# Attention of two layers with both heads of a pair at once: scores in 64x64 array tiles, weighing by P in 128x64 column tiles

## The chip, the core and the metric

The kernel runs on one core of one Trainium2 chip. The metric is the device time of one execution in microseconds (us), and smaller is better. TensorE is called PE below, VectorE DVE, ScalarE ACT, GpSimd POOL, and SyncE, which issues the loads of the weights, SP.

## The reference, cut to what matters

The program computes a first block of four layers and a second block of one. Layers 0 and 3 of the first block mix with dilated attention, and only that mixer is touched. There are 256 tokens and 1024 features, and 16 heads of 64 features, each with three groups of q, k and v (dilations 1, 4 and 16).

```python
ATTN_GROUPS = ((128, 1), (512, 4), (2048, 16))

def dilated_attention_mixer(x, positions, w_qkv, w_o):
    qkv = (x @ w_qkv).reshape(B, S, 3, GH, HEAD_DIM)
    q = rope_partial(qkv[:, :, 0], cos, sin)
    k = rope_partial(qkv[:, :, 1], cos, sin)
    v = qkv[:, :, 2]
    for g, (window, dilation) in enumerate(ATTN_GROUPS):
        sl = slice(g * HEADS_PER_GROUP, (g + 1) * HEADS_PER_GROUP)
        o, l = dilated_group_attention(q[:, :, sl], k[:, :, sl], v[:, :, sl], window, dilation)
        outs.append(o)
        lses.append(l)
    alpha = jax.nn.softmax(jnp.stack(lses, axis=0), axis=0)
    o = jnp.sum(alpha[..., None] * jnp.stack(outs, axis=0).astype(jnp.float32), axis=0)
    return o.astype(x.dtype).reshape(B, S, ATTN_OUT_WIDTH) @ w_o
```

The softmax over the groups' log-sum-exps makes the three groups of a head one softmax over all their keys, and the kernel computes it so: one row of scores per query, one maximum, one sum.

## The kernel before, in words

All large products are made three times, with both operands split into a rounded part and what rounding left (hi and lo, lines 225 to 227 in mm3). Weights come as units through SP's queue into one of three raw buffers, ACT rounds them to hi (line 73) and DVE subtracts (line 76); there are four buffers of hi and lo.

An attention layer (attn_layer) works through eight pairs of heads, s = 0 to 7. The 256 tokens are two tiles, T = 0 and 1, of 128 each. Within a tile even tokens come before odd ones, so that the second and the third group each keep to one half, c = 0 or 1, of 64 queries. The projections of the next pair (gemm(s + 1)) are a generator that yields after every 12 products of 128x384, 12 times per pair, and the attention steps of the pair are hung into these slots by number (the dictionary events, filled by at(slot, step, ...)). With b = 12 s - 1, the three flip_qk steps (transposes of q and k into qkT, line 782) stand in slots b to b + 2. Each pair has four units u = 4 s + i, i = 2 T + hh, where hh is the head of the pair. A unit has four steps:

- scores (slot b + 3 i + 3): the first group's scores by one product over 64 rows and 128 columns of the array (line 798), the other two groups' by four products of 64x64, for each half c and group g (line 803), all into one PSUM bank. DVE adds the mask and takes the maximum (line 807), ACT takes the exponential and its sum (line 808), DVE the reciprocal (line 809).
- flip_p (two slots later): the transposes of P (line 817), two for T = 0 and four for T = 1, and ACT's copy to pT (line 819).
- weigh (one slot after flip_p): P times v. The first group is one or two full 128x128 products (line 827), the others are 128x64 column tiles, one column tile for each c (line 831). DVE scales by the reciprocal into half of osb (line 832).
- flip_o, after the second head of a token tile: one transpose of osb (line 837), and hi and lo of the output (hid).

Steps of one slot stand in the order in which the loops append them, so in slot b + 6 the weighing of unit 0 comes directly before the scores of unit 1, and so on. What is left of the last units (the list tail: flip_p and weigh of u = 30 and 31, flip_o) runs within the boundary to the next phase (Boundary.run, argument mid), between the end of the first token tile's output projection and the transposes of the next norm (line 306). A scheduler then sets the order on each engine by its own estimates, with the written order as its basis.

All temporary PSUM results rotate through four banks (tp_bank), accumulators through four others (acc_bank).

## Time and profile before

| | us |
|---|---|
| median of three runs | 2191.24 |
| lowest, highest | 2190.22, 2191.39 |
| span of the profiled execution | 2182.7 |
| PE busy in it | 2153.9 |
| DVE busy in it | 1523.4 |
| ACT busy in it | 1219.5 |

The runs' times include what lies around the span, 8.5 us at the median. In the rows of a timeline, the first two columns are the start and the time from the first start to the last end of what is merged in the row, so rows can overlap: matmuls are pipelined, and what a piece of work takes in line is the distance from its start to the start of the next row. A form such as 64*128 64x256 says that 64 rows by 128 columns of the array hold the weights, and 256 columns are streamed through 64 rows. The count of a float32 product is twice the number of the program's instructions, since each is recorded as two passes. Products of hi and lo parts, and transposes, have one.

### The profile page before, as it was taken

To read this page: it belongs to the slowest core of one execution; us is meant where nothing else is said; L and a number is where in the kernel's file an instruction comes from. 1 tells how busy PE (TensorE), PEld (TensorE's weight loads), DVE (VectorE), ACT (ScalarE), POOL (GpSimd) and SP (SyncE) were. 2 spreads that over 40 slices of the span, in tenths; PEclk is the share of its full clock that TensorE was granted. 3 is DMA by queue.
4 is the path that set the end of the run, shared out by engine and by line. 5 is a ranking of instruction groups with operands and counts; after the bars stand their busy time and mean duration, and the time that the engine had idled before them with its cause. 6 is when DMAs were issued, how large, how long until landed. Compare 5 with 4: busy or idle time off the path is not lost.

```text
span 2182.7 us, 39068 instructions
## 1 busy us (share of the span) xinstructions
PE 2153.9 (99%) x15262; PEld 2007.8 (92%) x15262; DVE 1523.4 (70%) x3710; ACT 1219.5 (56%) x2355; POOL 94.8 (4%) x130
## 2 busy tenths in 40 slices
PE   9999999999999999999999999999999999989999
PEld 8999989989999889799889999899989998969999
DVE  6655569957799669799665555589757655677763
ACT  6555566645476566576555555576554445665442
POOL 1000000000000001100000000000010002011000
PEclk9999999999999999999999999999999999999999
DMA  7444436554555553155544434445537445423543
GB/s 256 141 132 133 160 108 213 184 188 155 199 179 199 193 182 112 39 180 198 193 161 149 144 131 133 152 157 193 193 139 260 165 155 180 150 68 125 185 156 116
DMA packets 57433, 352.33 MB, mean 161 GB/s; under 512 B 7233, under 2 KB 7777, under 8 KB 29729
## 3 DMA queue, kind: packets, MB, share of 16 engines
q1 hardware_dynamic: 53136, 338.88, 45.0%
q0 software_dynamic: 3824, 10.78, 1.6%
q8 instruction: 120, 1.97, 0.4%
q14 instruction: 65, 0.52, 0.1%
q10 hardware_dynamic: 288, 0.18, 0.0%
HBM read 348.74 MB, written 3.22 MB: 161 GB/s over the span
## 4 chain that ended last, share of the span: by engine, by line
PE 56%; DVE 5%; ACT 1%; POOL 1%; issue 1%; POOLq 0%; ACTq 0%; DVEq 0%
PE acc L225 16%; PE acc L227 16%; PE acc L226 16%; DVE lo L76 1%; DVE cvh L1015 1%; DVE o L1015 1%; PE tp L798 1%; PE tp L803 1%; POOL s L243 1%; PE tp L1664 1%; PE tp L782 1%; PE tp L817 0%; PE tp L831 0%; PE tp L992 0%; PE tp L827 0%
## 5 line engine op out<-in xcount | busy, mean ns | idle before, releaser
L76 DVE TENSOR_TENSOR lo<-raw,hi 128x512 fp32r<-128x512 f32 (+2 forms) x1440 | 855.1, 632 | 298.4 <-ACT hi L73 294.0
L73 ACT ACTIVATE hi<-raw 128x1024 fp32r<-128x1024 f32 (+3 forms) x720 | 670.2, 964 | 417.8 <-PE acc L226 156.5
L225 PE MATMUL acc<-xhi,hi 128*128 128x256 f32 (+1 forms) x2432 | 688.0, 283 | 0.9 <-DVE u L515 0.5
L227 PE MATMUL acc<-xhi,lo 128*128 128x256 f32 (+1 forms) x2432 | 688.3, 283 | 0.0
L226 PE MATMUL acc<-xlo,hi 128*128 128x256 f32 (+1 forms) x2432 | 688.0, 283 | 0.0
L225 PEld LDWEIGHTS acc<-xhi,hi 128*128 128x128 f32 x2432 | 459.5, 189 | 2.1 <-ACT u L513 0.7
L227 PEld LDWEIGHTS acc<-xhi,lo 128*128 128x128 f32 x2432 | 460.0, 189 | 1.1 <-issue 0.9
L226 PEld LDWEIGHTS acc<-xlo,hi 128*128 128x128 f32 x2432 | 457.1, 188 | 0.8 <-issue 0.4
L225 PE MATMUL acc<-hi,xhi 128*128 128x384 f32 (+2 forms) x920 | 321.3, 349 | 1.5 <-ACT xhi L348 1.4
L227 PE MATMUL acc<-hi,xlo 128*128 128x384 f32 (+2 forms) x920 | 307.7, 334 | 0.0
L226 PE MATMUL acc<-lo,xhi 128*128 128x384 f32 (+2 forms) x920 | 306.4, 333 | 0.0
L225 PE MATMUL acc<-hi,hidh 128*128 128x512 f32 x480 | 191.6, 399 | 0.6 <-ACT hidh L230 0.6
L226 PE MATMUL acc<-lo,hidh 128*128 128x512 f32 x480 | 189.6, 395 | 0.0
L227 PE MATMUL acc<-hi,hidl 128*128 128x512 f32 x480 | 189.5, 395 | 0.0
L225 PEld LDWEIGHTS acc<-hi,xhi 128*128 128x128 f32 x920 | 172.8, 188 | 10.9 <-ACT xhi L348 3.7
L226 PEld LDWEIGHTS acc<-lo,xhi 128*128 128x128 f32 x920 | 173.3, 188 | 1.9
L227 PEld LDWEIGHTS acc<-hi,xlo 128*128 128x128 f32 x920 | 172.7, 188 | 2.3
L243 POOL TENSOR_TENSOR s<-s,neghalf 128x1 f32<-128x1 f32 (+5 forms) x56 | 42.3, 757 | 1596.9 <-DVE s L256 1468.5
L225 PEld LDWEIGHTS acc<-hi,hidh 128*128 128x128 f32 x480 | 90.4, 188 | 20.9 <-issue 0.9
L227 PEld LDWEIGHTS acc<-hi,hidl 128*128 128x128 f32 x480 | 90.4, 188 | 20.3
L226 PEld LDWEIGHTS acc<-lo,hidh 128*128 128x128 f32 x480 | 90.5, 189 | 18.5
L225 PE MATMUL acc<-hidh,hi 128*128 128x272 f32 (+1 forms) x352 | 100.6, 286 | 0.0
(342 smaller groups left out, 2638.0 us busy)
## 6 DMA issues: line engine op xcount, KB each, us to landing
raw<-in_ffn_w_in_dram SPq DMA_DIRECT2D x88, 1024.0 KB, 4.9
raw<-in_attn_w_qkv_dram SPq DMA_DIRECT2D x96, 768.0 KB, 4.3
raw<-in_ffn_w_out_dram SPq DMA_DIRECT2D x44, 1024.0 KB, 4.9
raw<-in_ffn_w_gu_dram SPq DMA_DIRECT2D x44, 1024.0 KB, 4.9
raw<-in_ffn_w_dn_dram SPq DMA_DIRECT2D x32, 704.0 KB, 4.1
raw<-in_sc_w_in_dram SPq DMA_DIRECT2D x16, 768.0 KB, 4.3
raw<-in_cc_w_pw_dram SPq DMA_DIRECT2D x12, 1024.0 KB, 4.9
raw<-in_attn_w_o_dram SPq DMA_DIRECT2D x8, 1024.0 KB, 5.0
```

What stands on the lines that cost most here:

```text
L73: nc.scalar.activation(hi[:, sl], raw[:, sl], AF.Copy)
L76: nc.vector.tensor_sub(lo[:, s2], raw[:, s2], hi[:, s2].bitcast(F32))
L225: nc.tensor.matmul(o, lhsT=lh[0], rhs=rh[0], start=first, stop=False)
L226: nc.tensor.matmul(o, lhsT=lh[0], rhs=rh[1], start=False, stop=False)
L227: nc.tensor.matmul(o, lhsT=lh[1], rhs=rh[0], start=False, stop=last)
L243: mark["pow"] = nc.gpsimd.tensor_tensor(r[:parts], m[:parts], neghalf[:parts, :w], op=ALU.pow)
L782: nc.tensor.transpose(tp[:, 256 * c2 + P * T:256 * c2 + P * T + P], qk[s, T][:, 2 * c:2 * c + 2, :].rearrange("p a b -> p (a b)"), ident)
L798: nc.tensor.matmul(sc[:, 0:nw], lhsT=t[rows, 0, ts_], rhs=t[rows, 3, 0:nw], start=True, stop=True)
L803: nc.tensor.matmul(half[:, g], lhsT=t[rows, 1 + g, P * T + 64 * c:P * T + 64 * c + 64], rhs=keys, start=True, stop=True)
L1015: nc.vector.scalar_tensor_tensor(d, x, w, other, op0=ALU.mult, op1=ALU.add)
L1664: nc.tensor.matmul(o[:, :P], lhsT=pT[:rows, i, :], rhs=vals[t][:rows, P * hd:P * hd + P], start=i == 0, stop=i == len(kts) - 1)
```

## The change

Both heads of a pair and token tile are now one step. scores(s, T) takes two banks, one for each head, and makes twelve products of 64x64 tiles: for the first group one per head and half c, over all nw keys (line 802; before one product of 64x128 per head), and for the other two groups as before (line 808). The loops run over hh and c innermost, so each product goes to another of the four quarters of the array than the one before it: head hh has its 64 features in partitions 64 hh, the half c of the queries goes to output partitions 64 c. weigh(s, T) makes all products in 128x64 column tiles, the first group's too, with c innermost (line 840), both heads into one bank; one DVE operation scales both (line 843), and there is one reciprocal for both (line 818). There are four buffers for ns instead of two, and three for pT instead of two. The steps' slots are new: scores at b + 3 and b + 9, flip_p four slots after the scores, weigh two slots after flip_p, flip_o one after weigh. The steps of T = 1 run into the next pair's slots. The diff also drops docstrings and comments all over the file, which are left out here.

```diff
-            for f, u in mid:
-                f(u)
+            for f, a in mid:
+                f(*a)
...
-        def scores(u):
-            s, T, hh = unit(u)
-            t, ts_, rows = qkT[s], slice(P * T, P * T + P), slice(64 * hh, 64 * hh + 64)
-            nw = P * (T + 1)
-            sc = tp_bank()
-            nc.tensor.matmul(sc[:, 0:nw], lhsT=t[rows, 0, ts_], rhs=t[rows, 3, 0:nw], start=True, stop=True)
-            for c in range(2):
-                half = sc[64 * c:64 * c + 64, nw:2 * nw].rearrange("p (t g u) -> p g t u", g=2, u=64)
-                for g in range(2):
-                    keys = t[rows, 4 + g, 0:nw].rearrange("p (t c u) -> p c t u", c=2, u=64)[:, c]
-                    nc.tensor.matmul(half[:, g], lhsT=t[rows, 1 + g, P * T + 64 * c:P * T + 64 * c + 64], rhs=keys,
-                                     start=True, stop=True)
-            ns = pool.tile([P, 512], F32, tag="ns", bufs=2, name=nm("ns"))
-            nmax, den, rd = small(), small(), small()
...
+        def scores(s, T):
+
+            t = qkT[s]
+            nw = P * (T + 1)
+            sc = [tp_bank() for _ in range(2)]
+            tiles = [(hh, c) for hh in range(2) for c in range(2)]
+
+            def part(hh, c):
+                return sc[hh][64 * c:64 * c + 64], t[64 * hh:64 * hh + 64], P * T + 64 * c
+
+            for hh, c in tiles:
+                o, x, q0 = part(hh, c)
+                nc.tensor.matmul(o[:, 0:nw], lhsT=x[:, 0, q0:q0 + 64], rhs=x[:, 3, 0:nw], start=True, stop=True)
+            for g in range(2):
+                for hh, c in tiles:
+                    o, x, q0 = part(hh, c)
+                    half = o[:, nw:2 * nw].rearrange("p (t g u) -> p g t u", g=2, u=64)
+                    keys = x[:, 4 + g, 0:nw].rearrange("p (t c u) -> p c t u", c=2, u=64)[:, c]
+                    nc.tensor.matmul(half[:, g], lhsT=x[:, 1 + g, q0:q0 + 64], rhs=keys, start=True, stop=True)
+            den, rd = small(2), small(2)
...
-        def weigh(u):
-            s, T, hh = unit(u)
-            if hh == 0:
-                osb[s, T] = pool.tile([P, P], F32, tag="osb", bufs=2, name=nm("osb"))
+        def weigh(s, T):
             o = tp_bank()
-            for t in range(T + 1):
-                nc.tensor.matmul(o[:, :64], lhsT=pT[u][:, t, :], rhs=v[s, t][:, hh, :], start=t == 0, stop=False)
-            for c in range(2):
-                rows = slice(64 * c, 64 * c + 64)
-                for t in range(T + 1):
-                    nc.tensor.matmul(o[rows, :64], lhsT=pT[u][:, T + 1 + t, rows], rhs=vx[s, t][:, c, hh, :], start=False, stop=t == T)
-            nc.vector.tensor_scalar(osb[s, T][:, 64 * hh:64 * hh + 64], o[:, :64], sm_[u][1], None, op0=ALU.mult)
+            for hh in range(2):
+                steps = [(t, v[s, t][:, hh, :], None) for t in range(T + 1)]
+                steps += [(T + 1 + t, vx[s, t], hh) for t in range(T + 1)]
+                for i, (j, vals, h2) in enumerate(steps):
+                    for c in range(2):
+                        rows = slice(64 * c, 64 * c + 64)
+                        nc.tensor.matmul(o[rows, 64 * hh:64 * hh + 64], lhsT=pT[s, T][hh][:, j, rows],
+                                         rhs=vals if h2 is None else vals[:, c, hh, :], start=i == 0, stop=i == len(steps) - 1)
...
+            if s:
+                at(b + 1, flip_p, s - 1, 1)
+                at(b + 3, weigh, s - 1, 1)
+                at(b + 4, flip_o, s - 1, 1)
+            at(b + 3, scores, s, 0)
+            at(b + 7, flip_p, s, 0)
+            at(b + 9, weigh, s, 0)
+            at(b + 9, scores, s, 1)
+            at(b + 10, flip_o, s, 0)
+        tail += [(f, (7, 1)) for f in (flip_p, weigh, flip_o)]
```

On PE, the first layer, first pair, before: the weighing of the first head of T = 1 and the scores of the second (tp is the PSUM bank written, v and vx are the values, pT the transposed P).

```order
L827 MATMUL tp_835<-v_497,pT_813 128x64
L827 MATMUL tp_835<-v_516,pT_813 128x64
L831 MATMUL tp_835<-vx_498,pT_813 64x64
L831 MATMUL tp_835<-vx_517,pT_813 64x64
L831 MATMUL tp_835<-vx_498,pT_813 64x64
L831 MATMUL tp_835<-vx_517,pT_813 64x64
L798 MATMUL tp_843<-qkT_533 128x256
L803 MATMUL tp_843<-qkT_533 64x2x64 x4
```

On PE now: the weighing of T = 1 of the first pair, with the scores of the second pair's T = 0 behind it.

```order
L840 MATMUL tp_936<-v_497,pT_885 64x64 x2
L840 MATMUL tp_936<-v_516,pT_885 64x64 x2
L840 MATMUL tp_936<-vx_498,pT_885 64x64 x2
L840 MATMUL tp_936<-vx_517,pT_885 64x64 x2
L840 MATMUL tp_936<-v_497,pT_892 64x64 x2
L840 MATMUL tp_936<-v_516,pT_892 64x64 x2
L840 MATMUL tp_936<-vx_498,pT_892 64x64 x2
L840 MATMUL tp_936<-vx_517,pT_892 64x64 x2
L802 MATMUL tp_955<-qkT_838 64x128 x2
L802 MATMUL tp_956<-qkT_838 64x128 x2
L808 MATMUL tp_955<-qkT_838 64x64 x2
L808 MATMUL tp_956<-qkT_838 64x64 x2
```

Where three forms followed each other (full array, column tiles, 64x128 and then 64x64), there are two, and each row's x2 is the pair of column tiles.

On ACT, first layer, from the second to the third pair, before: the copies of P of T = 1 (pT) between halves of weight splits (hi), evacuations of v (v, vx), the copy of transposed q and k (qkT) and the exponential (ns).

```order
L73 ACTIVATE hi_1255<-raw_1111 128x768
L819 ACTIVATE pT_1184<-tp_1179 128x512
L73 ACTIVATE hi_1255<-raw_1111 128x768
L715 ACTIVATE v_1198<-acc_1139,s_244 128x128
L715 ACTIVATE vx_1199<-acc_1139,s_244 64x128 x2
L788 ACTIVATE qkT_1227<-tp_1228 128x512
L808 ACTIVATE ns_1220,s_1222<-ns_1220,s_1221 128x512
L715 ACTIVATE v_1246<-acc_1140,s_260 128x128
L715 ACTIVATE vx_1247<-acc_1140,s_260 64x128
L73 ACTIVATE hi_1310<-raw_1169 128x768 x2
L715 ACTIVATE vx_1247<-acc_1140,s_260 64x128
L819 ACTIVATE pT_1288<-tp_1283 128x512
```

Now, at the same place:

```order
L73 ACTIVATE hi_1299<-raw_1180 128x768
L829 ACTIVATE pT_1256<-tp_1251 128x512
L715 ACTIVATE vx_1229<-acc_1151,s_260 64x128
L829 ACTIVATE pT_1263<-tp_1258 128x512
L73 ACTIVATE hi_1299<-raw_1180 128x768
L788 ACTIVATE qkT_1209<-tp_1279 128x512
L73 ACTIVATE hi_1385<-raw_1235 128x768 x2
L815 ACTIVATE ns_1342,s_1340<-ns_1342,s_1343 128x256
```

The two copies of P, which stood eleven rows apart, are next to each other but for one small copy.

On PE, at the end of the second attention layer, before: the tail between products of the output projection (acc).

```order
L817 MATMUL tp_15806<-ident,ns_15693 128x128 x4
L225 MATMUL acc_15663<-hi_15624,hidh_12844 128x512
L226 MATMUL acc_15663<-lo_15625,hidh_12844 128x512
L227 MATMUL acc_15663<-hi_15624,hidl_12845 128x512
L225 MATMUL acc_15663<-hi_15624,hidh_12844 128x512
L827 MATMUL tp_15814<-v_15482,pT_15811 128x64
L827 MATMUL tp_15814<-v_15530,pT_15811 128x64
L831 MATMUL tp_15814<-vx_15483,pT_15811 64x64
L831 MATMUL tp_15814<-vx_15531,pT_15811 64x64
L831 MATMUL tp_15814<-vx_15483,pT_15811 64x64
L831 MATMUL tp_15814<-vx_15531,pT_15811 64x64
L817 MATMUL tp_15822<-ident,ns_15742 128x128 x4
```

And now:

```order
L827 MATMUL tp_15804<-ident,ns_15702 128x128 x4
L827 MATMUL tp_15811<-ident,ns_15706 128x128 x4
L225 MATMUL acc_15661<-hi_15631,hidh_12844 128x512
L226 MATMUL acc_15661<-lo_15632,hidh_12844 128x512
L840 MATMUL tp_15818<-v_15486,pT_15809 64x64 x2
L840 MATMUL tp_15818<-v_15512,pT_15809 64x64 x2
L840 MATMUL tp_15818<-vx_15487,pT_15809 64x64 x2
L840 MATMUL tp_15818<-vx_15513,pT_15809 64x64 x2
L840 MATMUL tp_15818<-v_15486,pT_15816 64x64 x2
L840 MATMUL tp_15818<-v_15512,pT_15816 64x64 x2
L840 MATMUL tp_15818<-vx_15487,pT_15816 64x64 x2
L840 MATMUL tp_15818<-vx_15513,pT_15816 64x64 x2
```

The last two weighings with their transposes have become one step, and two projection products stand between transposes and weighing instead of four.

## Rows read from the trace of the kernel before

**Rows 1.** The page's first part: busy time, share of the span, instructions

```profile
PE 2153.9 (99%) x15262; PEld 2007.8 (92%) x15262; DVE 1523.4 (70%) x3710; ACT 1219.5 (56%) x2355; POOL 94.8 (4%) x130
```

**Rows 2.** Stretch, us; busy PE, PEld, DVE, ACT, POOL; granted clock, DMA share, GB/s

```profile
66.89:102.04 35.15, 35.15 (x247) 32.97 (x247) 20.16 (x56) 19.43 (x38) 0.00 (x0) 1.00 0.42 136
```

**Rows 3.** PE's timeline, 85.3 to 87.2 us: start, us, line, operands, form, count

```profile
85.29 0.33 PE L227 MATMUL acc<-hi,xlo 128*128 128x384 f32 x1
85.46 0.33 PE L827 MATMUL tp<-v,pT 128*128 128x64 f32 x2
85.72 0.34 PE L831 MATMUL tp<-vx,pT 128*64 128x64 f32 x4
85.98 0.48 PE L798 MATMUL tp<-qkT 64*128 64x128 f32 x2
86.39 0.46 PE L803 MATMUL tp<-qkT 64*64 64x64 f32 x8
86.78 0.44 PE L225 MATMUL acc<-hi,xhi 128*128 128x384 f32 x1
87.06 0.34 PE L226 MATMUL acc<-lo,xhi 128*128 128x384 f32 x1
```

**Rows 4.** PE's timeline, 93.3 to 95.5 us

```profile
93.37 0.33 PE L827 MATMUL tp<-v,pT 128*128 128x64 f32 x2
...
93.89 0.70 PE L798 MATMUL tp<-qkT 64*128 64x256 f32 x2
94.52 0.66 PE L803 MATMUL tp<-qkT 64*64 64x128 f32 x8
95.11 0.44 PE L225 MATMUL acc<-hi,xhi 128*128 128x384 f32 x1
```

**Rows 5.** PE's timeline, 76.8 to 79.3 us

```profile
77.07 0.55 PE L827 MATMUL tp<-v,pT 128*128 128x64 f32 x4
77.55 0.46 PE L831 MATMUL tp<-vx,pT 128*64 128x64 f32 x8
77.94 0.48 PE L798 MATMUL tp<-qkT 64*128 64x128 f32 x2
...
78.74 0.44 PE L225 MATMUL acc<-hi,xhi 128*128 128x384 f32 x1
```

**Rows 6.** PE's timeline, 66.6 to 69.8 us

```profile
66.90 0.55 PE L827 MATMUL tp<-v,pT 128*128 128x64 f32 x4
...
68.98 0.66 PE L782 MATMUL tp<-ident,qk 128*128 128x128 f32 x4
```

**Rows 7.** PE's timeline in the second block, 1877.7 and 1881.1 us

```profile
1877.76 0.52 PE L1690 MATMUL tp<-kaT,qaT 64*128 64x144 f32 x4
1878.21 0.38 PE L225 MATMUL acc<-xhi,hi 128*128 128x256 f32 x1
...
1881.21 0.76 PE L1690 MATMUL tp<-kaT,qaT 64*128 64x144 f32 x8
1881.90 0.39 PE L225 MATMUL acc<-xhi,hi 128*128 128x256 f32 x1
```

**Rows 8.** ACT's groups in one pair of heads: busy us, mean ns, idle before

```profile
L808 ACT ACTIVATE ns<-ns,s 128x512 f32<-128x512 f32 x2 | 1.4, 724 | 0.4 <-DVE s L807 0.4
...
L819 ACT ACTIVATE pT<-tp 128x512 f32<-128x512 f32 x2 | 1.2, 590 | 0.6 <-PE tp L817 0.6
```

**Rows 9.** What line 827 (weighing) waited for in the whole span: us, times

```profile
  ACT pT L819: 1.2, 4
```

**Rows 10.** PE's timeline at the first attention layer's end, 313.4 to 315 us

```profile
313.44 0.39 PE L225 MATMUL acc<-hi,hidh 128*128 128x512 f32 x1
313.67 0.40 PE L226 MATMUL acc<-lo,hidh 128*128 128x512 f32 x1
314.28 0.65 PE L306 MATMUL tp<-ident,xs 128*128 128x128 f32 x4 [0.21 <-ACT xs L332]
```

**Rows 11.** The page's second part: GB/s moved in 40 slices of the span

```profile
GB/s 256 141 132 133 160 108 213 184 188 155 199 179 199 193 182 112 39 180 198 193 161 149 144 131 133 152 157 193 193 139 260 165 155 180 150 68 125 185 156 116
```

## The prediction

> **What bounds the kernel now.** I read the busy times first: TensorE (PE) is busy 99% of the span [rows 1]. [...] The third view is PE's timeline around the attention products, where the start of one row to the start of the next is what that row costs in line [rows 3 to 6]. A 128x384 projection product starts every 0.17 us [rows 3]; 144 of them (3 parts, 2 halves, 2 token tiles, 4 k, 3 each) are 25.06 us at 0.174. The other 10.09 us of the period are attention. Of these, 24 transposes of q, k and P and two of the output stay as they are; the rest, scores and weighing, is what changes.

> **What that rest costs before.** Four times a pair, PE goes from projections into weighing, then scores, then back. With 0.11 us for the first projection after it (0.28 to the next instead of 0.17 [rows 3]) the four cost: weighing of T = 0 with scores of T = 0: 86.78 - 85.46 + 0.11 = 1.43 [rows 3]; with scores of T = 1: 95.11 - 93.37 + 0.11 = 1.85 [rows 4]; weighing of T = 1 with scores of T = 0: 78.74 - 77.07 + 0.11 = 1.78 [rows 5]; with scores of T = 1, running on into transposes (half of the 0.11): 68.98 - 66.90 + 0.05 = 2.13 [rows 6]. Sum 7.19 us a pair.

> **Unit prices.** Every float32 product stands in the trace as two passes (x8 for the four products of L803). One tile at a time: L798's two passes take 0.41 for 128 columns [rows 3] and 0.63 for 256 [rows 4], so 0.11 a pass per 128 columns. Two column tiles: L803's eight passes take 0.39 for 64 columns [rows 3] and 0.59 for 128 [rows 4], 0.20 for 512 more columns where L798 took 0.22 for 256 more. The two column tiles therefore already run side by side, although all products of c = 0 stand ahead of those of c = 1 in the program. L831: two pairs of passes 0.26 [rows 3], four pairs 0.39 [rows 5], so 0.065 a pair; L803's pairs of 64 columns grow by 0.05; I take 0.06. L827 in the full array: two more passes take 0.22 (0.48 against 0.26 [rows 5, 3]), 0.11 a pass of 64 columns, which as a stream need 0.055: it waits for its 128-column weight load. Row tiles side by side are nowhere in these layers, but L1690 of the second block alternates two of them: four passes of 144 columns take 0.45 to the next row, eight take 0.69 [rows 7]: 0.24 for 576 columns more, half of L798's price. Row tiles overlap too, where the program alternates them. Four tiles at once no row shows; the pairwise rows are the nearest, and I take four.

> **The change part by part.** *Weighing* both heads in column tiles: 16 pairs of passes for T = 1, 8 for T = 0: 0.26 + 14 x 0.06 = 1.10 and 0.26 + 6 x 0.06 = 0.62; the full-array form with its 0.11 a pass is gone, and with it the change of form inside. *Scores* in four tiles: each tile has two passes over all keys and four over half of them. T = 0: 0.39 (four of 64, [rows 3]) + 2 x 0.11 = 0.61; T = 1: 0.59 + 2 x 0.22 = 1.03. *Changes of array form*: sixteen a pair become six. The one from weighing to scores and the way back lie in the prices above; the way in from projections to column tiles is not in the trace: 0 as into L827 at 85.46, or 0.15 as from L827 to L831 (0.26 less two streams of 0.055) [rows 3]; I take 0.10. Sum: 0.10 + 1.10 + 0.61 + 0.11 = 1.92 and 0.10 + 0.62 + 1.03 + 0.11 = 1.86, together 3.78 instead of 7.19: 3.41 us less a pair, 54.6 us for 16 pairs in two layers.

> *Off PE.* DVE loses half of the reciprocals and of the output scalings (one of both heads each); ACT's exponentials and copies stay, 0.72 and 0.59 us for T = 1 [rows 8], but come two by two. Hidden cover: from flip_p to weigh it was one slot of 12 products, now two, 24 x 0.174 = 4.2 us, in which ACT has two copies, 1.18 us, with a half of a weight split and a small copy between them. Scores to flip_p: two slots became four. Before, PE waited there only 1.2 us in four places [rows 9]. The new shares, 19.43 and 20.16 of 31.7 us, are 61 and 64%. The weights for a pair then arrive at 136 x 35.15 / 31.74 = 151 GB/s, and the page has a slice at 260 [rows 11]. Buffers (ns 4, pT 3) and banks (14 a pair instead of 17 from the same four) are freed two slots or more before their next use. If that cover is gone, it is the rival on waits below. SP's and POOL's orders do not change.

> *The tail.* After the last projections of a layer the transposes of the next norm wait for ACT: these products follow each other by 0.23 us, the last before the transposes starts at 313.67, and the transposes begin at 314.28 [rows 10], 0.4 us late. The chain of norm steps behind it does not get shorter, so what the last weighing saves, some 0.9 us a layer, turns into wait: 2 us back. Net 52.6.

> The profiled span is 2182.7, so 2130.1; the runs' median is 8.5 above the span, which I keep: 2191.2 - 52.6 = **2138.6**. Its own range: entry free (-3.2), pairs at 0.05 (24 x 0.01 x 16 = -3.8), no loss in the tail (-2): 2129.6; entry 0.15 (+1.6), pairs at 0.065 (+1.9), scattered waits (+5): 2147.

> **Rivals.** *Two tiles at once, not four*: the array overlaps column tiles in 64x64 form, but takes row tiles in turn. Then T = 0 costs 4 x 0.05 + 2 x 0.11 = 0.42 more, T = 1 0.84 more: 1.26 x 16 = 20.2, 2159. Against: [rows 7], in the 64x128 form. [...]

> *Weight loads in the open.* If a column tile's load does not hide behind the other tile's product, each of 24 pairs and 12 groups of four a pair pays the half of L827's 0.11: 36 x 0.055 x 16 = 31.7 more, 2170. For it: L827 waits for its loads. Against it: L831's 0.065 a pair holds two loads and two streams of 0.055. [...]

> *Waits for the softmax*: both heads' copies are needed at once. At 0.3 (a wait of [rows 9]) to 0.59 (one copy, [rows 8]) for each of 32 weighings: 9.6 to 19 more, 2148 to 2158.

> *No overlap when tiles alternate* (the other side). Before, one column tile's products all precede the other's; now each product goes to another tile than the last. If that keeps them apart, a pair costs 24 x 2 x 0.055 = 2.64 to weigh, 1.76 + 3.52 for scores and 1.02 of changes, 8.94 instead of 7.19: +28, 2219. It decides once less than a third of the 5.2 us of overlap comes. Against: L1690 alternates and overlaps [rows 7].

> *Nothing moves*: something else than PE sets the period, about 2191; against it [rows 2].

> **How the numbers follow.** Forecast 0.75, two tiles 0.10, waits 0.06, loads 0.03, no overlap 0.04, nothing 0.02. The range runs from the forecast's low end to the two-tile case: 2130 to 2160. About 0.2% is what a measurement tells from no change: faster 0.94, same 0.02, slower 0.04.

> **What would show it.** A steady pair period near 31.7 us with PE busy throughout; weigh and scores groups of 1.9 us each; scores of T = 1 near 1.0 (1.9 if only two tiles run), passes in fours a few ns apart; 16 pairs of weigh passes in 1.1 (2.0 with open loads); PE waiting for P's copies would show as idle before the weighing; the wait before the norm's transposes near 1.3 us. Wrong is the forecast if the period stays over 33 us.

## The result, and the profile after

The changed kernel takes 2134.82 us, the median of four runs (2131.56 to 2138.26), beside 2191.31 for the kernel before in the same comparison: a ratio of 0.9744, with a 95% interval of 0.973 to 0.9758. The forecast was 2138.6 with a range of 2130 to 2160. Run again with the experiments (label a0_changed), the changed kernel took 2136.38 against 2190.34, 0.9754 (0.9739 to 0.9769).

The first rows of the profile after that answer to [rows 1] and [rows 2] are the page's busy times, and a stretch of one pair of heads in the first attention layer, from the weighing at 170.10 to the same weighing of the next pair at 201.81. The columns of the second are the stretch, its length, busy PE, PEld, DVE, ACT, POOL, granted clock, DMA share, GB/s.

```profile
PE 2104.3 (99%) x15582; PEld 1974.8 (93%) x15582; DVE 1507.8 (71%) x3646; ACT 1216.2 (57%) x2355; POOL 95.5 (4%) x130
```

```profile
170.09:201.80 31.71, 31.71 (x267) 30.51 (x266) 19.21 (x51) 19.10 (x38) 0.00 (x0) 1.00 0.44 150
```

PE is busy 99% of the span in both kernels, which says nothing of the 50 us between them. The stretch says it: a pair took 35.15 us [rows 2] and takes 31.71, and PE still has no gap in it.

In the timeline of PE after, the weighing of T = 1 with the scores of T = 0, and below it the weighing of T = 0 with the scores of T = 1, answer to [rows 3 to 6]. As there, what a piece takes in line is the distance from its start to the start of the next row.

```profile
169.83 0.34 PE L227 MATMUL acc<-hi,xlo 128*128 128x384 f32 x1
170.10 0.45 PE L840 MATMUL tp<-v,pT 128*64 128x64 f32 x8
170.38 0.40 PE L840 MATMUL tp<-vx,pT 128*64 128x64 f32 x8
170.61 0.40 PE L840 MATMUL tp<-v,pT 128*64 128x64 f32 x8
170.84 0.40 PE L840 MATMUL tp<-vx,pT 128*64 128x64 f32 x8
171.18 0.45 PE L802 MATMUL tp<-qkT 64*64 64x128 f32 x8
171.45 0.41 PE L808 MATMUL tp<-qkT 64*64 64x64 f32 x16
171.79 0.45 PE L225 MATMUL acc<-hi,xhi 128*128 128x384 f32 x1
172.07 0.34 PE L226 MATMUL acc<-lo,xhi 128*128 128x384 f32 x1
```

```profile
153.10 0.33 PE L227 MATMUL acc<-hi,xlo 128*128 128x384 f32 x1
153.36 0.34 PE L840 MATMUL tp<-v,pT 128*64 128x64 f32 x4
...
153.98 0.66 PE L802 MATMUL tp<-qkT 64*64 64x256 f32 x8
154.46 0.62 PE L808 MATMUL tp<-qkT 64*64 64x128 f32 x16
155.01 0.45 PE L225 MATMUL acc<-hi,xhi 128*128 128x384 f32 x1
```

The first group takes 1.08 for the 32 passes of the weighing (170.10 to 171.18) and 0.61 for the 24 of the scores (171.18 to 171.79). With 0.10 on the way in (0.27 from L227 to L840 instead of 0.17) and 0.11 on the way out (0.28 from L225 to L226) it is 1.90 us. The second takes 0.62 and 1.03, 1.85 us in all. Unmerged, the records show the scores' passes starting in fours 6 to 7 ns apart, the next four 109 ns later for 128 columns, and the weighing's in pairs 6 to 7 ns apart, a pair every 58 ns.

Where the time went is seen by cutting each trace at the starts of PE's 100th, 1800th, 6300th and 7900th product of lines 225 to 227, counted from zero (there are 12744 in each of these kernels). Between the first two cuts lies nearly all of the first attention layer, between the last two nearly all of the second. The rest begins with 149.5 us that still belong to the first block (149.5 to 149.6 in all twelve traces); behind them comes the second block. Times are us. "Before, again" is the kernel before, profiled once more (label b0_before).

| | span | start to 100th | attention 1 | between | attention 2 | rest |
|---|---|---|---|---|---|---|
| before | 2182.7 | 28.9 | 356.5 | 726.8 | 357.0 | 713.5 |
| before, again | 2189.6 | 31.0 | 356.8 | 727.2 | 357.0 | 717.5 |
| after | 2132.8 | 30.2 | 329.4 | 726.4 | 329.8 | 717.1 |
| after, again (a0_changed) | 2133.2 | 29.4 | 329.3 | 726.8 | 329.7 | 718.0 |

The two attention layers lost 27.1 and 27.2 us, 54.4 together, where the forecast had 52.6 net. Everything else is the same within what one kernel differs from itself. PE's visits to the attention products account for it: they cost 7.19 us a pair before, as the prediction adds them up, and 3.75 after, which is 55.0 us for 16 pairs, less some 1 us that comes back at the layers' ends (see the tail below).

### The profile page after: what moved, and what is told of

Same layout as the page of the kernel before. It is cut to its first block, busy times and chain, and to the rows that moved or that the text cites. A ratio compares the mean times of both kernels' runs of the same rounds, so it can differ in the third digit from the quotient of the medians.

```text
span 2132.8 us, 39626 instructions
## 1 busy us (share of the span) xinstructions
PE 2104.3 (99%) x15582; PEld 1974.8 (93%) x15582; DVE 1507.8 (71%) x3646; ACT 1216.2 (57%) x2355; POOL 95.5 (4%) x130
## 4 chain that ended last, share of the span: by engine, by line
PE 56%; DVE 5%; ACT 1%; POOL 1%; issue 1%; ACTq 0%; POOLq 0%; DVEq 0%
PE acc L225 17%; PE acc L227 17%; PE acc L226 17%; DVE lo L76 1%; DVE cvh L1024 1%; DVE o L1024 1%; POOL s L243 1%; PE tp L1673 1%; PE tp L840 1%; PE tp L782 0%; PE tp L1001 0%; PE tp L827 0%; PE tp L802 0%; PE tp L306 0%; ACT hi L73 0%
## 5 line engine op out<-in xcount | busy, mean ns | idle before, releaser
L227 PE MATMUL acc<-xhi,lo 128*128 128x256 f32 (+1 forms) x2432 | 690.4, 284 | 0.0
L226 PE MATMUL acc<-xlo,hi 128*128 128x256 f32 (+1 forms) x2432 | 690.1, 284 | 0.0
L225 PE MATMUL acc<-xhi,hi 128*128 128x256 f32 (+1 forms) x2432 | 689.8, 284 | 0.2 <-DVE u L515 0.2
L227 PEld LDWEIGHTS acc<-xhi,lo 128*128 128x128 f32 x2432 | 461.9, 190 | 1.1 <-issue 0.9
L225 PEld LDWEIGHTS acc<-xhi,hi 128*128 128x128 f32 x2432 | 461.4, 190 | 1.0 <-issue 0.4
L226 PEld LDWEIGHTS acc<-xlo,hi 128*128 128x128 f32 x2432 | 459.0, 189 | 1.0 <-issue 0.6
L225 PE MATMUL acc<-hi,xhi 128*128 128x384 f32 (+2 forms) x920 | 317.7, 346 | 1.5 <-ACT xhi L348 1.4
L227 PE MATMUL acc<-hi,xlo 128*128 128x384 f32 (+2 forms) x920 | 307.9, 335 | 0.0
L226 PE MATMUL acc<-lo,xhi 128*128 128x384 f32 (+2 forms) x920 | 306.6, 333 | 0.0
L225 PE MATMUL acc<-hi,hidh 128*128 128x512 f32 x480 | 190.7, 398 | 0.3 <-ACT hidh L230 0.3
L227 PE MATMUL acc<-hi,hidl 128*128 128x512 f32 x480 | 189.6, 395 | 0.0
L226 PE MATMUL acc<-lo,hidh 128*128 128x512 f32 x480 | 189.4, 395 | 0.0
L225 PEld LDWEIGHTS acc<-hi,xhi 128*128 128x128 f32 x920 | 172.8, 188 | 9.8 <-ACT xhi L348 3.2
L227 PEld LDWEIGHTS acc<-hi,xlo 128*128 128x128 f32 x920 | 172.7, 188 | 2.5
L226 PEld LDWEIGHTS acc<-lo,xhi 128*128 128x128 f32 x920 | 173.2, 188 | 1.9
L225 PEld LDWEIGHTS acc<-hi,hidh 128*128 128x128 f32 x480 | 90.5, 189 | 20.6 <-ACT hidh L230 0.5
L227 PEld LDWEIGHTS acc<-hi,hidl 128*128 128x128 f32 x480 | 90.4, 188 | 19.7
L226 PEld LDWEIGHTS acc<-lo,hidh 128*128 128x128 f32 x480 | 90.5, 188 | 19.3
L225 PE MATMUL acc<-hidh,hi 128*128 128x272 f32 (+1 forms) x352 | 100.6, 286 | 0.0
```

What stands on the lines that cost most here:

```text
L225: nc.tensor.matmul(o, lhsT=lh[0], rhs=rh[0], start=first, stop=False)
L226: nc.tensor.matmul(o, lhsT=lh[0], rhs=rh[1], start=False, stop=False)
L227: nc.tensor.matmul(o, lhsT=lh[1], rhs=rh[0], start=False, stop=last)
```

## The experiments

Shares of one edit are told below by the two attention stretches of the traces, which repeat within 0.3 us, and by the medians with their intervals. The first four runs (a0_changed and e1 to e3) stood beside the kernel before at 2190.34 us, the next four at 2189.69, the last two at 2190.25.

**The changed kernel again.** Nothing is edited; it is the standard for the rest.

> The changed kernel itself, to see how its span goes with the granted clock. In the first trace the two attention layers gave 53.3 us and the unchanged rest took 3.4 us back, all of it where the granted clock stood at 0.5 in the second block's mixer. Theory: the work in the attention layers takes the same time in every run, and runs differ by the clock in the unchanged part; a run whose mean clock is 0.001 higher is about 2 us shorter. Rival: the runs differ although the mean clock does not.

Measured: 2136.38 us, attention layers 329.3 and 329.7, the same as in the first trace to 0.1 us, as the theory has it. (The 53.3 us that it names are 54.4 by the table's cuts.) How the time goes with the mean clock these four runs cannot tell, since theirs is 0.992 or 0.993 throughout. The four runs of the first comparison can: from 2138.26 us at 0.992 to 2131.56 at 0.996 it is 1.7 us for 0.001, near the 2 expected.

**One part alone: weighing in column tiles, one head at a time.** The kernel before, with this edit:

```diff
-            for t in range(T + 1):
-                nc.tensor.matmul(o[:, :64], lhsT=pT[u][:, t, :], rhs=v[s, t][:, hh, :], start=t == 0, stop=False)
-            for c in range(2):
-                rows = slice(64 * c, 64 * c + 64)
-                for t in range(T + 1):
-                    nc.tensor.matmul(o[rows, :64], lhsT=pT[u][:, T + 1 + t, rows], rhs=vx[s, t][:, c, hh, :], start=False, stop=t == T)
+            for j in range(2 * (T + 1)):
+                for c in range(2):
+                    rows = slice(64 * c, 64 * c + 64)
+                    vals = v[s, j][:, hh, :] if j <= T else vx[s, j - T - 1][:, c, hh, :]
+                    nc.tensor.matmul(o[rows, :64], lhsT=pT[u][:, j, rows], rhs=vals, start=j == 0, stop=j == 2 * T + 1)
```

> The kernel before, with all weighing in column tiles, one head at a time, in the old slots; scores as before. Theory (0.06 us per pair of passes, 0.10 for the way in instead of 0.15 from the full array): T = 0 saves 0.04 us a unit, T = 1 0.145, 0.37 a pair of heads, 6 us in all: 2185. Rival, weight loads of column tiles in the open: 0.055 more for each of 24 pairs of passes, 21 us more than that, slower than before: 2206.

Measured: 2183.34 us, ratio 0.9969 (0.9957 to 0.998); the attention layers lost 3.1 us each. PE's timeline of this run, at the place of [rows 5]:

```profile
79.09 0.45 PE L830 MATMUL tp<-v,pT 128*64 128x64 f32 x8
79.37 0.40 PE L830 MATMUL tp<-vx,pT 128*64 128x64 f32 x8
79.71 0.48 PE L798 MATMUL tp<-qkT 64*128 64x128 f32 x2
```

The weighing takes 0.62 us (79.09 to 79.71) where it took 0.87 before (77.07 to 77.94 [rows 5]). Against this stands the way into column tiles: from the last projection product to the first pass it is 0.27 us here (78.82 to 79.09), where it was 0.17 into the full array (76.90 to 77.07). So the column tiles in place of the full array's products are worth 6 us of the 54, as expected, and no more.

**One part alone: scores in 64x64 tiles, one head at a time.** The kernel before, with the first group's product split in two and c made the inner loop:

```diff
-            nc.tensor.matmul(sc[:, 0:nw], lhsT=t[rows, 0, ts_], rhs=t[rows, 3, 0:nw], start=True, stop=True)
             for c in range(2):
-                half = sc[64 * c:64 * c + 64, nw:2 * nw].rearrange("p (t g u) -> p g t u", g=2, u=64)
-                for g in range(2):
+                q0 = P * T + 64 * c
+                nc.tensor.matmul(sc[64 * c:64 * c + 64, 0:nw], lhsT=t[rows, 0, q0:q0 + 64], rhs=t[rows, 3, 0:nw], start=True, stop=True)
+            for g in range(2):
+                for c in range(2):
+                    half = sc[64 * c:64 * c + 64, nw:2 * nw].rearrange("p (t g u) -> p g t u", g=2, u=64)
```

> The kernel before, with all scores in 64x64 tiles, one head at a time (two column tiles, one row tile), in the old slots; weighing as before. Theory: T = 0 takes 0.61 us instead of 0.80, T = 1 1.03 instead of 1.22, 0.19 each for 64 units: 12 us, 2179. Rival: the first group's product gains nothing from being halved, since both halves read the same keys: 2191.

Measured: 2177.95 us, ratio 0.9945 (0.993 to 0.996); the attention layers lost 5.7 us each, 11.5 together, near the 12 of the theory.

**Both parts, one head at a time.** The two edits together; what is missing of the change is that the heads come in pairs.

> Both edits of the forms, one head at a time in the old slots. Theory: the sum, 18 us, 2173; what is left to the changed kernel, about 36 us, then is the pairing of heads (four tiles at once, half as many ways in and out). Rival: the forms alone give most of it, below 2155.

Measured: 2170.26 us, ratio 0.9909 (0.9893 to 0.9926); the attention layers lost 18.9 us together. PE's timeline of this run, one head's weighing and one head's scores of T = 0:

```profile
86.69 0.34 PE L832 MATMUL tp<-v,pT 128*64 128x64 f32 x4
86.85 0.29 PE L832 MATMUL tp<-vx,pT 128*64 128x64 f32 x4
87.07 0.44 PE L800 MATMUL tp<-qkT 64*64 64x128 f32 x4
87.34 0.40 PE L805 MATMUL tp<-qkT 64*64 64x64 f32 x8
87.66 0.44 PE L225 MATMUL acc<-hi,xhi 128*128 128x384 f32 x1
```

The two forms give a third of the gain. The other 35.5 us (54.4 less 18.9) come with the pairing of the heads and its new slots, which the next run takes apart.

**The pair's scores in two tiles instead of four.** The changed kernel, with both heads' scores from the same rows of the array:

```diff
-                return sc[hh][64 * c:64 * c + 64], t[64 * hh:64 * hh + 64], P * T + 64 * c
+                return sc[hh][64 * c:64 * c + 64], t[0:64], P * T + 64 * c
```

> The changed kernel, but the scores of both heads are made from the first head's rows (the second head's scores are left out, the first's made twice), so that the four products of a round stand in two tiles of the array and not four; all else as it was. Theory: only two tiles run at once, T = 0 takes 0.42 us longer and T = 1 0.84, 1.26 a pair of heads, 20 us: 2155. Rival: row tiles do not run side by side in 64x64 form anyway or something else gave the gain: 2135.

Measured: 2156.41 us, ratio 0.9838 (0.9822 to 0.9855); the attention layers take 339.6 and 340.2 us, 20.7 more than in the changed kernel. PE's timeline of this run, the scores of T = 0 and of T = 1:

```profile
77.96 0.65 PE L802 MATMUL tp<-qkT 64*64 64x128 f32 x8
78.44 0.63 PE L808 MATMUL tp<-qkT 64*64 64x64 f32 x16
79.00 0.44 PE L225 MATMUL acc<-hi,xhi 128*128 128x384 f32 x1
...
92.94 1.08 PE L802 MATMUL tp<-qkT 64*64 64x256 f32 x8
93.85 1.04 PE L808 MATMUL tp<-qkT 64*64 64x128 f32 x16
94.82 0.44 PE L225 MATMUL acc<-hi,xhi 128*128 128x384 f32 x1
```

The same products with the same columns take 1.04 and 1.88 us where four tiles take 0.61 and 1.03. So passes in four quarters of the array do run side by side here, and that is 20.7 us of the 35.5. The 14.8 left are argued from rows and not from a run of their own: per pair and token tile, two trips into attention become one. By the starts of its rows, a pair's visits cost 5.96 us with one head at a time (the run before) and 5.03 in this run, which is 14.9 us for 16 pairs, so next to nothing is left for the new slots and buffers. The rows also price a single trip. Two heads' weighings of T = 0 one by one are 2 x 0.38 (86.69 to 87.07 in the run before), together 0.62; two heads' scores in two tiles are 2 x 0.59 (87.07 to 87.66) one by one and 1.04 together. With 0.09 to 0.10 in and 0.11 out, one trip less is 0.14 + 0.14 + 0.10 + 0.11 = 0.49 us, and 32 of them 15.7, an estimate that comes out 0.9 high.

**The heads' scores one after the other.** The changed kernel with all six products of one head ahead of those of the other; the four tiles are the same:

```diff
-            for hh, c in tiles:
-                o, x, q0 = part(hh, c)
...
-            for g in range(2):
-                for hh, c in tiles:
+            for head in range(2):
+                mine = tiles[2 * head:2 * head + 2]
+                for hh, c in mine:
+                    o, x, q0 = part(hh, c)
...
+                for g in range(2):
+                    for hh, c in mine:
```

> The changed kernel with the scores' loops turned: all six products of the first head, then all six of the second, instead of head and half innermost. Theory: the array looks far enough ahead in its queue to start the second head's rows while the first head's still run, as it did with the halves before: 2135, the first products of the two heads some 40 ns apart. Rival: it works in order, and heads in turn run one after the other: up to 20 us more, 2155.

Measured: 2148.02 us, ratio 0.9807 (0.9793 to 0.9822); attention layers 335.3 and 335.9, 12.1 us more than in the changed kernel. Neither theory named this size. The queue is the expectation's word; what the trace shows is when passes start. PE's timeline of this run, the scores of T = 1 (L804 is the first product of each tile, L810 the other two):

```profile
156.89 0.65 PE L804 MATMUL tp<-qkT 64*64 64x256 f32 x4
157.38 0.28 PE L810 MATMUL tp<-qkT 64*64 64x128 f32 x2
157.39 0.43 PE L804 MATMUL tp<-qkT 64*64 64x256 f32 x2
157.48 0.39 PE L810 MATMUL tp<-qkT 64*64 64x128 f32 x4
157.66 0.38 PE L804 MATMUL tp<-qkT 64*64 64x256 f32 x2
157.70 0.77 PE L810 MATMUL tp<-qkT 64*64 64x128 f32 x10
158.40 0.44 PE L225 MATMUL acc<-hi,xhi 128*128 128x384 f32 x1
```

The second head's first passes (157.39) do not start with the first head's (156.89), and they do not wait for its last either. Each tile has six passes: two of L804 and four of L810. The second head starts 5 ns after the first head's two tiles have begun their third pass each (157.38, x2), that is, when three passes are left to start in each, and from there on passes of both heads start among each other (157.38 to 157.70). All 32 score groups of this trace have this order, for 128 columns (T = 0) as for 256.

**The halves of the queries one after the other.** The changed kernel with c as the outer loop of the weighing:

```diff
-                for i, (j, vals, h2) in enumerate(steps):
-                    for c in range(2):
-                        rows = slice(64 * c, 64 * c + 64)
+                for c in range(2):
+                    rows = slice(64 * c, 64 * c + 64)
+                    for i, (j, vals, h2) in enumerate(steps):
```

> The changed kernel with the weighing's loops turned: for each head all products of the half c = 0, then those of c = 1, instead of the halves in turn. Theory: as with the old line 831, the two column tiles run side by side all the same: 2135. Rival: they run one after the other: 24 times 0.05 us a pair of heads, 19 us more, 2154.

Measured: 2141.57 us, ratio 0.9773 (0.9758 to 0.9788); attention layers 332.5 and 333.0, 6.4 us more. Again neither theory named this size. PE's timeline of this run, the weighing of T = 1 (eight passes to the one column tile, eight to the other, for each head):

```profile
170.59 0.45 PE L840 MATMUL tp<-v,pT 128*64 128x64 f32 x4
170.87 0.22 PE L840 MATMUL tp<-vx,pT 128*64 128x64 f32 x1
170.88 0.27 PE L840 MATMUL tp<-v,pT 128*64 128x64 f32 x1
...
171.73 0.40 PE L840 MATMUL tp<-vx,pT 128*64 128x64 f32 x4
172.06 0.45 PE L802 MATMUL tp<-qkT 64*64 64x128 f32 x8
```

The other tile's first pass (170.88, L840 from v) starts 7 ns after the first tile's fifth of eight (170.87, from vx), again when three passes are left to start. The weighing takes 1.47 us instead of 1.08. The weighing of T = 0, whose runs are four passes long, lost only 0.04: its whole group takes 1.89 instead of 1.85. The two runs agree in a count, taken for each tile: the first pass for an idle tile started when three passes were left to start in each busy one, three in all where one tile was busy (e5), six where two were (e4). The kernel before fits it as well: its runs to one tile (L803, L831) are of four passes at most, and at 77.55 and 78.36 of its trace, unmerged, the two tiles' first passes start 13 ns apart. The theory of the next run is the author's estimate from these counts, which are of starts alone; no record shows a pass that waits.

**Runs of two products.** The changed kernel with the weighing in runs of two products, four passes:

```diff
-                for i, (j, vals, h2) in enumerate(steps):
+                for lo in range(0, len(steps), 2):
                     for c in range(2):
                         rows = slice(64 * c, 64 * c + 64)
-                        nc.tensor.matmul(o[rows, 64 * hh:64 * hh + 64], lhsT=pT[s, T][hh][:, j, rows],
...
+                        for i, (j, vals, h2) in list(enumerate(steps))[lo:lo + 2]:
+                            nc.tensor.matmul(o[rows, 64 * hh:64 * hh + 64], lhsT=pT[s, T][hh][:, j, rows],
```

> The changed kernel, with the weighing's products ordered in runs: two products (four passes) to the one column tile, two to the other, and so on, where e5_halves_in_turn gave up to four products (eight passes) in a row to one tile. Theory: a tile takes one running and three waiting passes, and only the fifth that comes while four are there holds up everything behind it. Runs of four passes then cost nothing: the group of T = 1's weighing takes 1.90 to 1.95 us as in the changed kernel, the attention layers 329.4 to 330.0 us, the median 2135 to 2138. Rival: there is no such limit, each run keeps the two tiles from overlapping in proportion to its length (0.38 us per group for runs of eight passes, nothing for runs of two): 0.13 us more in each of 16 groups, 2.03 us a group, 2 us more in all, attention layers 330.4.

Measured: 2136.35 us, ratio 0.9747 (0.973 to 0.9764); the group of T = 1 takes 1.93 us, that of T = 0 1.89; the attention layers take 330.4 and 330.8. PE's timeline of this run:

```profile
172.12 0.46 PE L841 MATMUL tp<-v,pT 128*64 128x64 f32 x8
172.40 0.45 PE L841 MATMUL tp<-vx,pT 128*64 128x64 f32 x8
...
173.25 0.45 PE L802 MATMUL tp<-qkT 64*64 64x128 f32 x8
```

The weighing takes 1.13 us: 0.05 more than in the changed kernel, not the 0.13 of the rival, and not the 0.38 of runs of eight. The group and the median lie where the theory put them. But the layers are 1.0 us longer, above the theory's 330.0 and at the 330.4 that the rival had named: runs of four cost some 0.04 us a group (16 groups in a layer, 0.6 us), and another 0.4 us a layer I cannot place. Unmerged, the second tile starts its last pass 54 ns behind the first; with c innermost both tiles' last passes start 7 ns apart. A run of four is nearly free, not free, and this run alone would not decide between the two; what speaks for a limit is where the idle tiles start in e4 and e5.

**The cover halved.** The changed kernel with flip_p one slot ahead of weigh instead of two:

```diff
-                at(b + 1, flip_p, s - 1, 1)
+                at(b + 2, flip_p, s - 1, 1)
...
-            at(b + 7, flip_p, s, 0)
+            at(b + 8, flip_p, s, 0)
```

> The changed kernel with flip_p one slot later, so one slot (12 products, 2.1 us) ahead of the weighing instead of two. Theory: ACT has two copies of 0.59 us and up to two halves of a weight split of 0.84 us in that time, so PE waits some tenths before the weighing: 0.3 us for one of two weighings a pair, 5 us, 2140. Rival: the second slot was not needed, 2135.

Measured: 2137.12 us, ratio 0.9757 (0.9742 to 0.9772); attention layers 329.7 and 329.7, 0.3 us more than in the changed kernel. What line 840 (weighing) waited for from ACT in the whole span (us, times), in this run and then in the changed kernel, answers to [rows 9]:

```profile
  ACT pT L829: 1.4, 4
```

```profile
  ACT hi L73: 0.7, 2
  ACT pT L829: 0.7, 2
```

In both it is 1.4 us in four places; in the changed kernel two of them are put down to another of ACT's operations. One slot, 2.1 us of projections, already hides ACT's two copies (0.59 us each for T = 1, 0.37 for T = 0 in the changed kernel's trace), as the rival had it. The second slot changes nothing that the medians can show.

**The kernel before, profiled again.** Nothing is edited. The question was what the 8.5 us between the first profile's span and the median were.

> The kernel before, profiled again; nothing is changed in it. Question: what are the 8.5 us by which the median of its runs lies over the span of its first profile? Theory: they are not around the span. Every run of the kernels so far exceeds its own span by 1.9 us, so an ordinary run of the kernel before has a span of 2186 to 2190 at a mean granted clock of 0.993 to 0.996, and the profile shows where: stretches at a granted clock of 0.5 in the second block, whose mixer is the same in both kernels, while the four layers of the first block take the same as in the first profile (attention layers 356.5 and 357.0 us from their 100th to their 1800th projection product). Rival: the second block keeps the full clock in this kernel and the span is again 2182 to 2184; then the change itself brings the slow stretches into the second block and costs 3 to 4 us there.

Measured: 2191.49 us with a span of 2189.6, 1.9 us apart. The core's span and mean granted clock in this run (2182.7 and 0.997 in the first profile of before), and then two stretches of the second block in the first profile and in this one (columns as in [rows 2]):

```profile
core 0: 2189.6 us, clock 0.993
```

```profile
1920.00:1930.00 10.00, 9.99 (x58) 7.45 (x58) 7.76 (x36) 6.52 (x27) 0.93 (x1) 1.00 0.01 2
1990.00:2000.00 10.00, 9.66 (x78) 9.27 (x79) 7.52 (x18) 5.08 (x8) 1.25 (x3) 1.00 0.56 198
```

```profile
1920.00:1930.00 10.00, 9.19 (x42) 7.68 (x44) 4.80 (x22) 3.81 (x17) 1.18 (x2) 0.66 0.10 43
1990.00:2000.00 10.00, 8.42 (x60) 8.22 (x59) 9.04 (x19) 5.38 (x11) 4.46 (x6) 0.84 0.31 105
```

The theory holds in the main. The same program had a granted clock of 1.00 throughout both stretches in one execution, and of 0.66 and 0.84 on the mean in the other (the work stands some 3 us later in it), and the rest, with the second block, took 717.5 us instead of 713.5. That is 4.0 of the 6.9 us between the two spans. Another 2.1 lie before the 100th product, which the theory did not name: from 10.3 to 13.7 us the granted clock is 0.51 in this run and 1.00 in the first. The changed kernel's profile has the like in its second block:

```profile
1860.00:1890.00 30.00, 26.53 (x118) 18.36 (x119) 21.02 (x101) 17.00 (x60) 4.57 (x5) 0.83 0.17 54
```

So the slow stretches are not the change's doing. What brings the clock down there in one execution and not in another stays open.

## Why the prediction was right, by its steps

**The bound.** Right: PE's products set the end of the attention stretches, and what they lost the span lost. The period of which the prediction gives 10.09 us to attention is the stretch of [rows 2], one pair of heads in 35.15 us with PE busy in all of it. The steady period is now 31.71 us (31.7 forecast), PE busy in all of it.

**The unit prices.** Right, nearly to the hundredth:

| | forecast | measured |
|---|---|---|
| weighing of T = 1, of T = 0 | 1.10, 0.62 | 1.08, 0.62 |
| scores of T = 0, of T = 1 | 0.61, 1.03 | 0.61, 1.03 |
| way in, way out | 0.10, 0.11 | 0.10, 0.11 |
| the two groups | 1.92, 1.86 | 1.90, 1.85 |
| a pair of column tiles' passes | 0.06 | 0.058 |

Two values had no row of their own. Four tiles at once were taken from the rows of two tiles, and those held. The way in was set at 0.10 between its bounds of 0 and 0.15 without a row that says so; that it came out at 0.09 to 0.10 is in part luck. The traces show what it is. In front of the full array's products the first load starts 0.17 us ahead of its pass, beside the last projection product (85.29 and 85.46 in the kernel before); in front of column tiles it starts with the pass (170.09 and 170.10 in the changed kernel), 0.25 us after the end of the load before it. It is so in all 32 groups of the changed kernel.

**Off PE.** Right: DVE and ACT are busy 61 and 60% of the period (64 and 61 forecast; it is DVE that lost work), and the weights arrive at 150 GB/s (151 forecast). Half of the cover named for the copies of P was enough (e6). Of the counts beside it one is a slip on which nothing rests: a pair takes 15 temporary banks now (three for q and k, four for scores, four for P, two each for weighing and output), not 14.

**The tail.** Right in its mechanism, wrong in its size. The weighings' gain in a layer's tail was to become wait before the norm's transposes, 0.9 us a layer. The transposes after, and what PE's idle time before L306 ended with at the first layer's end (us, times), after and then before:

```profile
287.57 0.40 PE L227 MATMUL acc<-hi,hidl 128*128 128x512 f32 x1
288.44 0.66 PE L306 MATMUL tp<-ident,xs 128*128 128x128 f32 x4 [0.47 <-ACT xs L332]
```

```profile
  ACT xs L332: 1.4, 2
```

```profile
  ACT xs L332: 0.9, 2
```

Idle for the two sets of transposes rose from 0.9 to 1.4 us, by 0.5 and not 0.9; the first set is late by 0.87 less 0.23, 0.64 us, where it was 0.4 [rows 10] and 1.3 were forecast. The term of 2 us should have been 1. The rest of the way from 52.6 to 54.4 is the 0.03 us by which the two groups came out shorter (0.5 us), and 0.3 us that I cannot put to a row. The other 2 us between 2138.6 and 2134.8 are the spread of the runs: the changed kernel's second median is 2136.4, 54.0 below the kernel before beside it.

**The base.** Wrong in what it was called, right in the sum. "8.5 above the span, which I keep" took the difference of the first profile to the median for time around the span. Around it lie 1.9 us; the other 6.6 are a first profile that happened to be a short execution (2182.7 beside 2189.6). Since the changed kernel's ordinary runs are long in the same two columns of the table (30.2 and 717.1 us in its first trace), subtracting from the median was right all the same, though not for the reason given; had the short execution's span been held against the changed kernel's own span, the gain would have read 49.9 us.

**The range.** Its term for pairs of passes at 0.05 us counts 24 pairs, where the forecast prices 20 at 0.06 (14 and 6). By those the low end is 0.6 us higher and the high end 0.3 lower, which changes nothing.

**The rivals.** Two tiles instead of four, priced at 20.2 us more, cost 20.7 when the kernel was made to run so (e7): the price was right and the case did not occur. Weight loads in the open would have cost 36 x 0.055 us a pair. The row of half of the weighing's loads in the changed kernel's trace (count; shortest, median and longest in ns; first and last start) says the contrary:

```profile
L840 PEld LDWEIGHTS tp<-v,pT x384: 132/138/138, 58.2 to 1367.8; 128*64 128x64 f32 x192
```

There is a load for each pass, recorded with 138 ns, and still a pair of passes starts every 58 ns. Both column tiles use all 128 rows. In the full array of the kernel before, unmerged, L827's second pass at 77.07 starts 55 ns after the first, and the next two 110 and 112 ns after the pass ahead of them, where their loads start 108 and 111 ns apart; that is the wait for loads that the prediction reads into L827's 0.11. Waits for the softmax are the 1.4 us above, in the whole span. No overlap when tiles alternate was the rival of the other side, and the experiments turn it over: tiles that alternate overlapped here, and long runs to one tile cost (e4 12.1 us, e5 6.4).

## What to carry to other kernels

When small products sit between large ones in another array form, price the round trip first: here some 0.49 us each beyond the passes themselves, and halving the trips was worth 14.8 us where running four tiles instead of two was worth 20.7. Give each product to another tile than the last one; here two float32 products (four passes) in a row to one tile cost little (0.05 us a weighing of T = 1 in e8), and three (e4, 12.1 us in all) or four (e5, 6.4) cost more. And before a span is set against a median, look whether the profiled execution is an ordinary one: the granted clock and the span of the other runs say so.

## What the runs showed of the hardware that was not expected

Passes of different tiles started out of the program's order: in e5 the first tile's later passes (from vx, 170.87 on) start among the second tile's (from v, 170.88 on).

In two stretches of the second block the granted clock fell to 0.66 and 0.84 on the mean of 10 us in one execution and stayed at 1.00 in another of the same program; the rest of the span was 4.0 us longer there in the kernel before. What follows the attention layers is the same in all kernels of this study: the rest from the 7900th product on took 713.5 and 713.7 us in two profiled executions (the first of before, and e5), and 715.6 to 718.0 in the other ten.
